# Two-block transformer kernel on one core: the second block's modulations made by TensorE in strips (layer 0) and by VectorE alone (last layer)

## The chip, the core and the metric

The kernel runs on one core of one Trainium2 chip. The core has a matrix engine (TensorE, PE in the profile, with its weight loads as PEld), a vector engine (VectorE, DVE), a scalar engine (ScalarE, ACT), GpSimd (POOL) and SyncE (SP), which issues most of the transfers. The metric is the device time of one execution in microseconds; lower is better.

## The reference, cut to what matters

A first block (three mixers, cross attention to `mem`, a convolutional feed-forward layer) is followed by a second block of two layers: attention and SwiGLU, then a recurrence (HGRN) and SwiGLU. Each layer of the second block is modulated: shifts, scales and gates for its 512 tokens come from the vector `c`, those for its 256 context tokens from `c_ctx`.

```python
for i in range(DEPTH_2):
    mod_l = (jax.nn.silu(c) @ ada_w[i] + ada_b[i])[:, None, :]           # 1024 -> 6 * 1024
    mod_c = (jax.nn.silu(c_ctx) @ ada_w[i] + ada_b[i])[None, None, :]
    sh1_l, sc1_l, gt1_l, sh2_l, sc2_l, gt2_l = jnp.split(mod_l, 6, axis=-1)
...
    hn_l = modulate(rms_norm_2(h, norm_mix_w[i]), sh1_l, sc1_l)           # h * (1 + sc) + sh
...
    h = h + gt1_l * y_l
    h = h + gt2_l * swiglu(modulate(rms_norm_2(h, norm_ffn_w[i]), sh2_l, sc2_l), ffn_w_in[i], ffn_w_out[i])
```

`ada_w` is 1024 x 6144 for each layer, 24 MiB in float32. Two vectors are multiplied with it, so a layer's modulations are two matrix-vector products.

## The kernel before

**Matrix products.** Activations lie with features on partitions. A product is made from two parts of each float32 operand, a high part of the reduced type `fp32r` and the rest: `Stream.weights` (L190) loads 128 columns of weights (512 KB) into one of three `raw` buffers, ScalarE rounds them to `wh` (L196), VectorE subtracts to give `wl` (L200), and `Stream.multiply` (L229) issues three `fp32r` products for each of the 8 tiles of the contraction (L236). `parts` has two buffers, so the weights of one tile are prepared while TensorE works on another. In a stage's last products (`closing`, L266) GpSimd makes half of each `wl`.

**Stages that the change touches.** The first block's feed-forward layer, `conv_ffn` (L1319), goes over 22 pairs of column tiles; each pair's two products pass ScalarE (L1331) and four VectorE steps (L1332, L1333), then the gate (L1349 to L1351) and the two parts (L335, L336); after 8, 8 and 6 pairs follow the products with `ffn_w_down`. The second block's layer 0 then has the projections, the attention `attend` (L1647), its output product, and `swiglu` (L1524), which is built as `conv_ffn` is, without the convolution and for 768 tokens. Layer 1's `swiglu`, the last stage, has the same for 512 tokens.

**The modulations.** `modulations(b, l, mod)` (L1458) is a generator; a step is one of 48 groups of 128 outputs, with the outputs on partitions and the 1024 inputs along the free dimension. It loads 512 KB of transposed weights `w` (L1477, two buffers) and makes a dot product with each of the two vectors, which are copied to all partitions. For layer 0 both go by GpSimd and ScalarE: GpSimd multiplies (L1484), ScalarE adds up (L1485). For layer 1 the first vector's product is one VectorE instruction with an accumulator (L1480); the second vector's, needed for the first 16 groups only, goes by GpSimd and ScalarE. Layer 0's run as `b.filler` beside `conv_ffn`, 2 or 3 steps for each pair of tiles (L1343), through `Context.steps` (L2022), which goes on to the context's first norm. Layer 1's run beside layer 0's `swiglu` (L1549). `Mod` (L1493) makes the norms' gains from the scales.

**Attention.** For each of 16 heads there are 7 steps: six with the 512 later tokens, one with the 256 context tokens. A step makes scores (L1719, L1720), the exponential (L1722), its two parts (L1728, L1729, on GpSimd, VectorE and ScalarE in turn) and, three steps later, the products with the values (L1741 to L1743). Beside them `ahead` (L1658) prepares the next two heads, with the queries' maxima sent by SP's queue (L1708, `q<-mr`), and `divide` (L1757) sends the sums by the same queue (L1760, `s<-sums`). Banks of PSUM for these side steps come from a pool `ps` of four. No weights are used between the projections and the output product.

**What sets the order.** A scheduler places the instructions when the program is built, by the order in which the generators are stepped, buffers and its own estimate of time. On each engine, and in SP's queue, they are then taken in that fixed order; one that waits holds back all behind it.

Of the kernel before, what the change touches and what calls it, by code (L numbers as in the profile page):

```python
# [26 lines left out]
# ---------------------------------------------------------------------------------------------  # L27
# Layout of the inputs, and constants of the shapes.


def _w(a):
    """[K, M] -> [M / 128, 128, K / 128, 128]: for each 128 columns, what each partition holds."""
    a = np.asarray(a)
    k, m = a.shape
    return np.ascontiguousarray(a.reshape(k // P, P, m // P, P).transpose(2, 1, 0, 3))


def _fm(a):
    """[tokens, features] -> [128, features / 128, tokens]."""
# [5 lines left out]
def _wt(a):  # L45
    """[K, M] -> [M / 256, K / 512, 128, 4, 256]."""
# [20 lines left out]
def _consts():  # L67
# [28 lines left out]
    out["half"] = np.full((P, 32), -0.5)  # L96
# [4 lines left out]
#: What all of the kernel needs, what the first block's mixers need, the second block's layers.  # L101
CGROUPS = {
    "all": ["ident", "half"],
# [6 lines left out]
def _layout(i):  # L110
# [26 lines left out]
    o["cc"] = np.ascontiguousarray(np.broadcast_to(np.stack([i["c_2"][0], i["c_ctx_2"]]), (P, 2, D)))  # L137
    o["ctx"] = _fm(i["ctx_2"][0])
    for l in range(2):
        o[f"ada{l}"] = np.ascontiguousarray(i["ada_w_2"][l].T.reshape(48, P, D))  # L140
        o[f"ffn_in{l}"] = _w(i["ffn_w_in_2"][l])
        o[f"ffn_out{l}"] = _w(i["ffn_w_out_2"][l])
# [26 lines left out]
# ---------------------------------------------------------------------------------------------  # L169


class Stream:
    """A stream of matrix products: its weights as loaded, their two parts, its accumulators."""
# [16 lines left out]
    def weights(self, src, ks, m=P, parts=None):  # L190
        """src [128, ks, m] in DRAM -> its high and low parts."""
# [11 lines left out]
    def accumulators(self, kinds):  # L203
        """For each (n, count): that many accumulators [128, n], of the same bank where they fit."""
# [12 lines left out]
    def products(self, W, ks, xs, n, ms, take, m=P, k0=0):  # L217
        """take(i, acc): acc [m, n] holds columns ms[i] of x W, features on partitions. A step for each i."""
# [6 lines left out]
    def product(self, src, ks, sets, m=P, k0=0):  # L225
        """For each (acc, xh, xl) of sets(k): acc += (rows k of the weights)^T x."""
# [1966 lines left out]
```

## Time and profile before

| what | value |
|---|---|
| three runs | 3298.18, 3301.41, 3302.06 us; median 3301.41 us |
| span of the profiled execution | 3296.8 us; what lies around it isn't in the profile, the median is 4.6 us above it |
| TensorE busy | 3096.2 us (94%) |
| VectorE, ScalarE, GpSimd busy | 1943.9, 1302.4, 1123.0 us |
| `conv_ffn`'s stretch read below | 953.6 to 1367.3 us |
| attention's stretch | 1540.2 to 1740 us |
| layer 0's `swiglu` beside the modulations | 1860 to 2050 us |
| layer 1's `swiglu`, same products as `conv_ffn` | 2906.2 to 3239.2 us |

The busy share of TensorE is an average over stages. A stretch is read by how much of it TensorE is not busy, by which engine ends those waits, and by the granted clock, of which the profile gives the share of full speed (2.4 GHz; the other level is 1.2 GHz).

### The profile page before, as it was taken

Reading aid. Unit: us, or ns where it says so; the run is one execution under the profiler, and the core shown is the slowest. Engines: PE = TensorE matmul, PEld = TensorE weight load, DVE = VectorE, ACT = ScalarE, POOL = GpSimd, SP = SyncE. Lnnn points to the kernel's source line nnn. Section 1 sums busy time; section 2 is a strip of 40 time slices with the busy share of each in tenths; the row PEclk is TensorE's granted clock in tenths of the full one; section 3 lists DMA queues with packets and bytes.
Section 4 is the critical chain, followed back from the end, with each engine's and each line's share of the span. In section 5 each row is a group of like instructions: output and inputs, shape, how many; then the busy total and the mean of one; then the engine's idle time right before and its main releaser. Section 6 shows DMA issues by size and latency. Waiting matters only on the chain.

```text
span 3296.8 us, 50925 instructions
## 1 busy us (share of the span) xinstructions
PE 3096.2 (94%) x20168; PEld 2640.3 (80%) x20168; DVE 1943.9 (59%) x3138; ACT 1302.4 (40%) x2333; POOL 1123.0 (34%) x942
## 2 busy tenths in 40 slices
PE   7999999989998889989999989999999999899998
PEld 6777777769796667888768968888889999788887
DVE  6454476456469695777975585333465555653334
ACT  4332234334345565544664331111344443332223
POOL 3222032230048988267975340000233232310003
PEclk9999999999999989999999999999999999989999
DMA  2111333234244444342003355221231111123333
GB/s 98 54 56 46 96 91 94 85 124 125 76 147 134 161 153 158 109 128 65 1 1 122 115 192 191 65 64 58 86 112 58 52 58 43 49 77 96 96 96 115
DMA packets 130911, 309.20 MB, mean 94 GB/s; under 512 B 33888, under 2 KB 55088, under 8 KB 130032
## 3 DMA queue, kind: packets, MB, share of 16 engines
q1 hardware_dynamic: 126032, 293.95, 28.6%
q10 hardware_dynamic: 4640, 12.00, 1.0%
q8 instruction: 158, 2.59, 0.3%
q14 instruction: 81, 0.66, 0.1%
HBM read 296.23 MB, written 8.39 MB: 92 GB/s over the span
## 4 chain that ended last, share of the span: by engine, by line
PE 68%; DVE 13%; POOL 6%; issue 5%; DMA 4%; ACT 3%; SPq 0%; POOLq 0%; DVEq 0%; ACTq 0%
PE acc L236 45%; DVE wl L200 4%; PE ps L520 3%; PE gate L1190 3%; POOL x L1484 2%; PE acc L258 2%; PE acc L259 2%; PE acc L260 2%; PE ps L1930 2%; DMA w<-in_ada_dram 2%; POOL pl L1729 1%; DVE t L1351 1%; DVE t L1350 1%; DVE junk L1480 1%; ACT wh L196 1%
## 5 line engine op out<-in xcount | busy, mean ns | idle before, releaser
L236 PE MATMUL acc<-hh,wl 128*128 128x512 f32 (+1 forms) x2296 | 772.5, 368 | 62.3 <-DVE wl L200 58.8
L236 PE MATMUL acc<-hh,wh 128*128 128x512 f32 (+1 forms) x2296 | 766.4, 365 | 0.0
L236 PE MATMUL acc<-hl,wh 128*128 128x512 f32 (+1 forms) x2296 | 764.2, 365 | 0.0
L200 DVE TENSOR_TENSOR wl<-raw,wh 128x1024 fp32r<-128x1024 f32 (+3 forms) x584 | 585.0, 1004 | 279.3 <-ACT wh L196 276.3
L196 ACT CAST wh<-raw 128x1024 fp32r<-128x1024 f32 (+4 forms) x584 | 479.9, 826 | 580.7 <-PE acc L236 356.4
L236 PEld LDWEIGHTS acc<-hh,wl 128*128 128x128 f32 x2296 | 408.3, 192 | 144.5 <-DVE wl L200 71.5
L200 POOL TENSOR_TENSOR wl<-raw,wh 128x512 fp32r<-128x512 f32 (+1 forms) x120 | 170.4, 1423 | 1014.5 <-ACT wh L196 579.9
L236 PEld LDWEIGHTS acc<-hh,wh 128*128 128x128 f32 x2296 | 407.1, 191 | 69.3 <-issue 1.1
L236 PEld LDWEIGHTS acc<-hl,wh 128*128 128x128 f32 x2296 | 407.5, 191 | 66.5 <-issue 0.8
L1484 POOL TENSOR_TENSOR x<-w,silu 128x1024 f32<-128x1024 f32 x112 | 323.7, 2918 | 46.1 <-ACT x L1485 23.0
L236 PE MATMUL acc<-mh,wl 128*128 128x512 f32 (+1 forms) x848 | 268.0, 341 | 26.7 <-DVE wl L200 26.4
L236 PE MATMUL acc<-mh,wh 128*128 128x512 f32 (+1 forms) x848 | 263.2, 336 | 0.0
L236 PE MATMUL acc<-ml,wh 128*128 128x512 f32 (+1 forms) x848 | 262.7, 335 | 0.4 <-DVE ml L336 0.4
L236 PEld LDWEIGHTS acc<-mh,wl 128*128 128x128 f32 x848 | 152.8, 191 | 51.0 <-DVE wl L200 33.6
L236 PEld LDWEIGHTS acc<-ml,wh 128*128 128x128 f32 x848 | 152.6, 190 | 19.1 <-DVE ml L336 1.7
L236 PEld LDWEIGHTS acc<-mh,wh 128*128 128x128 f32 x848 | 152.2, 190 | 17.1
L1509 DVE SCALAR_TENSOR_TENSOR X<-acc,mod,X 128x256 f32<-128x256 f32 (+1 forms) x112 | 65.6, 594 | 154.5 <-PE acc L236 154.5
L1557 ACT ACTIVATE t<-acc 128x512 f32<-128x512 f32 x66 | 34.5, 525 | 309.1 <-PE acc L236 307.8
L1485 ACT ACTIVATE x<-x 128x1024 f32<-128x1024 f32 x112 | 118.4, 1057 | 93.5 <-POOL x L1484 93.2
L1558 DVE SCALAR_TENSOR_TENSOR t<-t,acc 128x512 f32<-128x512 f32 x66 | 39.4, 596 | 169.2 <-ACT t L1557 169.1
L258 PE MATMUL acc<-wl,hh 128*128 128x256 f32 x448 | 126.8, 285 | 1.7 <-DVE wl L200 1.0
L259 PE MATMUL acc<-wh,hl 128*128 128x256 f32 x448 | 127.0, 284 | 0.0
(597 smaller groups left out, 6051.8 us busy)
## 6 DMA issues: line engine op xcount, KB each, us to landing
w<-in_ada_dram SPq DMA_DIRECT2D x96, 512.0 KB
raw<-in_ffn_in_dram SPq DMA_DIRECT2D x88, 512.0 KB
raw<-in_ffn_w_up_dram SPq DMA_DIRECT2D x44, 512.0 KB
raw<-in_ffn_out_dram SPq DMA_DIRECT2D x32, 512.0 KB
raw<-in_hg_w_dram SPq DMA_DIRECT2D x32, 512.0 KB
raw<-in_ffn_out_dram SPq DMA_DIRECT2D x40, 384.0 KB
raw<-in_w_qkv_dram SPq DMA_DIRECT2D x24, 512.0 KB
raw<-in_attn_wo_dram SPq DMA_DIRECT2D x24, 512.0 KB
```

Of the source, the lines that this page charges most:

```text
L196: nc.scalar.copy(h, raw)
L200: e.tensor_tensor(l[:, s], raw[:, s], h[:, s].bitcast(F32), op=ALU.subtract)
L236: nc.tensor.matmul(z[0], w[:, k], z[x], start=k == 0 and n == 0, stop=k == ks - 1 and n == 2)
L258: nc.tensor.matmul(acc, xh, wl, start=k == 0, stop=False)
L259: nc.tensor.matmul(acc, xl, wh, start=False, stop=False)
L260: nc.tensor.matmul(acc, xh, wh, start=False, stop=k == ks - 1)
L520: nc.tensor.matmul(out(r, ci), lhsT(r, ci), rhs(r, ci), start=start, stop=stop)
L1190: nc.tensor.matmul(acc, w[:, 0], x, start=k + i == 0, stop=k == 7 and i == 2)
L1484: nc.gpsimd.tensor_tensor(x, w, c[:, n], op=ALU.mult)
L1485: nc.scalar.activation(x, x, AF.Identity, accum_out=sums[:, g, n : n + 1])
L1509: return lambda i, acc: b.nc.vector.scalar_tensor_tensor(X[:, i], acc, gate[:, i : i + 1], X[:, i], op0=ALU.mult, op1=ALU.add)
L1930: nc.tensor.matmul(p[:, c], kc[:, c * P : (c + 1) * P], qc[:, c * P : (c + 1) * P], start=True, stop=True)
```

## The change

Layer 0's modulations are now matrix products. `silu` of the two vectors is put on partitions as a [128, 8, 32] tile, of which two columns are used and 30 are zero. A group is 512 outputs, 12 groups in all: 8 float32 products with a 128 x 32 stationary tile (`silu`) and 512 moving columns of weights, one for each tile of the contraction, into four strips of 32 PSUM partitions by `tile_position`. The weights come in four transfers of 512 KB for a group. ScalarE copies the bank, and four small products with `sel` add the strips and turn the outputs to partitions; VectorE adds the bias. Four groups (parts 0 and 1 of the modulations) run beside `conv_ffn`, one step for every second pair; eight run inside `attend`, a step for every seventh of its steps, and take their weights through the stream's three `raw` buffers and their bank from the pool of four. The last layer's modulations take VectorE for both vectors, with three buffers for `w`. The gain of the second norm is made later, by `second()`.

```diff
-    out["half"] = np.full((P, 32), -0.5)
+    out["half"] = np.full((P, 8), -0.5)
+    out["sel"] = p[:, None] % 32 == np.arange(2)[None]
...
-        o[f"ada{l}"] = np.ascontiguousarray(i["ada_w_2"][l].T.reshape(48, P, D))
+        ada = i["ada_w_2"][l]
+        o[f"ada{l}"] = np.ascontiguousarray(ada.T.reshape(48, P, D) if l else
+                                            ada.reshape(4, 2, P, 12, 512).transpose(3, 0, 2, 1, 4))
...
-                b.fill(2 + m % 2)
+                b.fill(m % 2)
...
+class Products:
+    def __init__(self, b, mod, pool, small):
+        self.b, self.mod = b, mod
+        nc = b.nc
+        self.silu = pool.tile([P, 8, 32], F32, name="silu")
+        c, t = (small.tile([P, 8, 2], F32, name=n) for n in ("cin", "cth"))
+        nc.scalar.dma_start(c, b.a["ck"])
+        nc.gpsimd.memset(self.silu, 0.0)
+        nc.scalar.activation(t, c, AF.Tanh, scale=0.5)
+        nc.vector.tensor_scalar(t, t, 0.5, 0.5, op0=ALU.mult, op1=ALU.add)
+        nc.vector.tensor_tensor(self.silu[:, :, :2], c, t, op=ALU.mult)
+    def steps(self, groups, bank, pool):
+        b, nc = self.b, self.b.nc
+        bias = b.v["ada_b_2"]
+        for g in groups:
+            acc = bank()
+            for k in range(8):
+                if k % 2 == 0:
+                    w = pool.tile([P, 2, 512], F32, tag="raw", name="ada")
+                    nc.sync.dma_start(w, b.a["ada0"][g, k // 2])
+                c = 32 * (k % 4)
+                nc.tensor.matmul(acc[c : c + 32], self.silu[:, k], w[:, k % 2], start=k < 4, stop=k >= 4,
+                                 tile_position=(0, c))
+            yield
+            sb = pool.tile([P, 512], F32, tag="raw", name="mods")
+            nc.scalar.copy(sb, acc)
+            for j in range(4):
+                nc.tensor.matmul(acc[:, 2 * j : 2 * j + 2], sb[:, j * P : (j + 1) * P], b.c["sel"], start=j == 0,
+                                 stop=j == 3)
+            s = slice(4 * g, 4 * g + 4)
+            nc.vector.tensor_tensor(self.mod[:, s], acc[:, :8].rearrange("p (j n) -> p j n", n=2),
+                                    bias[:, s].unsqueeze(2).to_broadcast([P, 4, 2]), op=ALU.add)
+            yield
...
-        p2 = b.pool("ad2", 2, ctx=ctx, side="right")
+        p2 = b.pool("ad2", 3, ctx=ctx, side="right")
...
-        nc.gpsimd.tensor_scalar(t, t, 0.5, 0.5, op0=ALU.mult, op1=ALU.add)
-        nc.gpsimd.tensor_tensor(c, c, t, op=ALU.mult)
+        nc.vector.tensor_scalar(t, t, 0.5, 0.5, op0=ALU.mult, op1=ALU.add)
+        nc.vector.tensor_tensor(c, c, t, op=ALU.mult)
...
-            for n in range(2 if l == 0 or g < 16 else 1):
-                if n == 0 and l:
-                    nc.vector.scalar_tensor_tensor(t[:, 0], w, 1.0, c[:, n], op0=ALU.mult, op1=ALU.mult,
-                                                   accum_out=sums[:, g, n : n + 1])
-                    continue
-                x = p2.tile([P, D], F32, tag="x", name="x")
-                nc.gpsimd.tensor_tensor(x, w, c[:, n], op=ALU.mult)
-                nc.scalar.activation(x, x, AF.Identity, accum_out=sums[:, g, n : n + 1])
+            for n in range(2 if g < 16 else 1):
+                nc.vector.scalar_tensor_tensor(t[:, 0], w, 1.0, c[:, n], op0=ALU.mult, op1=ALU.mult,
+                                               accum_out=sums[:, g, n : n + 1])
...
+        if i % 7 == 3:
+            next(more, None)
...
-        yield from modulations(b, 0, self.mod[0])
+        with ExitStack() as c:
+            self.products = Products(b, self.mod[0], cx, b.pool("cin", 1, ctx=c, side="right"))
+            ps, ada = b.pool("psad", 1, PSUM, ctx=c), b.pool("ada", 4, ctx=c, side="right")
+            yield from self.products.steps(range(4), lambda: ps.tile([P, 512], F32, tag="ps", name="mods"), ada)
...
+                more = old_.products.steps(range(4, 12), lambda: ps.tile([P, 512], F32, tag="ps", name="mods"), st.raw)
+                att = attend(b, Q, K2, V, o, high, low, at2, ps, c, more)
```

How the instructions stand is shown at three places. In the changed file the same code has other line numbers: L204 for L200, L240 for L236, L382 for L378, L351 for L347, L1754 for L1708, L1806 for L1760, L1765 and L1766 for L1719 and L1720, L1787 to L1789 for L1741 to L1743.

GpSimd in the stretch of `conv_ffn`, before: `x<-w,silu` is layer 0's product with a vector, on both sides of it stand its help with the weights' parts and the norms' sums.

```order
L200 TENSOR_TENSOR wl<-raw,wh 128x512 x5
L347 TENSOR_TENSOR rs<-rs,ct_all 128x2
L1470 TENSOR_SCALAR junk<-junk 128x2048
L1471 TENSOR_TENSOR silu<-silu,junk 128x2048
L1484 TENSOR_TENSOR x<-w,silu 128x1024 x96
L378 TENSOR_TENSOR sum<-sum,sq 128x256 x2
L347 TENSOR_TENSOR rs<-rs,ct_all 128x2
```

The same place after:

```order
L204 TENSOR_TENSOR wl<-raw,wh 128x512 x5
L351 TENSOR_TENSOR rs<-rs,ct_all 128x2
L1473 MEMSET silu 128x256
L382 TENSOR_TENSOR sum<-sum,sq 128x256 x2
L351 TENSOR_TENSOR rs<-rs,ct_all 128x2
```

The 96 products and the two steps for `silu` are gone from GpSimd; one memset stands in their place, and the engine has nothing else in this stretch.

TensorE in `attend`, before: `st` are scores, `acc` the products with the values, `sc` those for the maxima of the next heads.

```order
L1698 MATMUL sc<-K_13074,q_15043 128x384 x2
L1719 MATMUL st<-q_14780,K_14166 128x512
L1720 MATMUL st<-q_14778,K_13074 128x512
L1698 MATMUL sc<-K_13074,q_15043 128x384
L1719 MATMUL st<-q_14780,K_14166 128x512
L1720 MATMUL st<-q_14778,K_13074 128x512
```

The same place after, for the second of the eight groups: `mods<-ada,silu` are the products in strips.

```order
L1744 MATMUL sc<-K_12780,q_14773 128x384 x2
L1489 MATMUL mods<-ada,silu 32x512 x6
L1744 MATMUL sc<-K_12780,q_14773 128x384
L1765 MATMUL st<-q_14486,K_13872 128x512
L1766 MATMUL st<-q_14484,K_12780 128x512
...
L1744 MATMUL sc<-K_12780,q_14773 128x384
L1489 MATMUL mods<-ada,silu 32x512 x2
L1765 MATMUL st<-q_14486,K_13872 128x512
L1766 MATMUL st<-q_14484,K_12780 128x512
...
L1789 MATMUL acc<-ph,Vh 65x512
L1495 MATMUL mods<-ct_all,mods 128x2 x4
L1744 MATMUL sc<-K_12780,q_14774 128x384 x2
```

Six strips stand together, the last two 13 rows behind them, the four small products 15 rows further on; all are in TensorE's fixed order among the scores.

SP's queue in `attend`, before, with what each transfer waits for:

```order
L187 DMA raw<-in_attn_wo_dram 128x1024 [waits DMAHW4_49,DVE_49,Pool_49]
L1708 DMA q_14780<-mr 1x6x128 [waits Activation_49]
L1708 DMA q_14781<-mr 1x6x128
L1760 DMA s<-sums 6x1x128 [waits DVE_49,Activation_49,Pool_49]
L1760 DMA s<-sums 6x1x128 [waits DMAHW5_49,Activation_49]
L1760 DMA s<-sums 6x1x128 [waits DMAHW6_49,Activation_49]
```

After:

```order
L1487 DMA ada<-in_ada_dram 128x1024 [waits DMAHW3_49,PE_49]
L1487 DMA ada<-in_ada_dram 128x1024 [waits DMAHW5_49,PE_49]
L1487 DMA ada<-in_ada_dram 128x1024 [waits DMAHW0_49,PE_49]
L1487 DMA ada<-in_ada_dram 128x1024 [waits DMAHW4_49,PE_49,Activation_49]
L1806 DMA s<-sums 6x1x128 [waits DVE_49,Activation_49,Pool_49]
L1754 DMA q_14486<-mr 1x6x128 [waits Activation_49]
L1754 DMA q_14487<-mr 1x6x128 [waits DMAHW6_49]
L1806 DMA s<-sums 6x1x128 [waits DMAHW7_49,Activation_49]
L1487 DMA ada<-in_ada_dram 128x1024 [waits DMAHW1_49,PE_49]
```

The last transfer of a group and the first three of the next one now stand between the small transfers of the attention, and wait for TensorE (the strips that free a buffer) and once for ScalarE.

## Rows read from the trace of the kernel before

**Rows 1.** The page, part 1: engines, busy us and share of the span.

```profile
PE 3096.2 (94%) x20168; PEld 2640.3 (80%) x20168; DVE 1943.9 (59%) x3138; ACT 1302.4 (40%) x2333; POOL 1123.0 (34%) x942
```

**Rows 2.** Busy time by stretch: length, engines, granted clock, DMA share, GB/s.

```profile
953.60:1367.30 413.70, 363.88 (x1618) 293.54 (x1617) 314.95 (x280) 232.57 (x368) 294.58 (x109) 0.95 0.45 145
2906.20:3239.20 333.00, 331.32 (x1547) 278.89 (x1548) 137.66 (x173) 90.45 (x123) 2.97 (x4) 0.98 0.29 89
1540.20:1740.00 199.80, 188.58 (x907) 135.44 (x907) 155.95 (x263) 126.82 (x250) 176.35 (x178) 0.95 0.01 4
1860.00:2050.00 190.00, 170.54 (x936) 147.18 (x935) 133.97 (x176) 50.38 (x78) 57.18 (x18) 0.96 0.57 188
```

**Rows 3.** Groups by line, 965 to 1310 us: busy, mean ns, idle before.

```profile
L1484 POOL TENSOR_TENSOR x<-w,silu 128x1024 f32<-128x1024 f32 x96 | 273.9, 2883 | 30.8 <-ACT x L1485 21.7 <-DMA w<-in_ada_dram 8.9
...
L200 DVE TENSOR_TENSOR wl<-raw,wh 128x1024 fp32r<-128x1024 f32 x47 | 85.1, 1814 | 24.5 <-ACT wh L196 24.5
...
L1351 DVE TENSOR_TENSOR t<-t,u 128x512 f32<-128x512 f32 x16 | 41.7, 2603 | 0.0
```

**Rows 4.** The same view, 2880 to 3297 us, layer 1's `swiglu`.

```profile
L200 DVE TENSOR_TENSOR wl<-raw,wh 128x1024 fp32r<-128x1024 f32 (+2 forms) x79 | 84.9, 1075 | 21.2 <-ACT wh L196 21.0
...
L1559 DVE TENSOR_TENSOR t<-t,acc 128x512 f32<-128x512 f32 x22 | 15.1, 688 | 55.7 <-PE acc L236 55.7
```

**Rows 5.** Waits of TensorE, 953 to 1368 us: us, times, longest.

```profile
PE acc L236 <- DVE wl L200: 49.6, 28, 5.7
```

**Rows 6.** The chain of waits in order of time: start, us, what.

```profile
968.08 26.52 PE acc L236 x180
...
1329.17 38.13 PE acc L236 x168
...
1375.18 4.45 DMA raw<-in_ffn_w_down_dram
```

**Rows 7.** TensorE in order of time, first block's recurrence: start, us, instruction.

```profile
238.13 0.80 PE L520 MATMUL pp<-bt,AR 64*64 64x64 f32 x21
238.86 1.12 PE L555 MATMUL pp<-twd,up 64*128 64x512 f32 x2
239.91 0.50 PE L1190 MATMUL gate<-hh,wl 128*128 128x512 f32 x1
240.25 0.39 PE L1190 MATMUL gate<-hl,wh 128*128 128x512 f32 x1
240.47 0.40 PE L1190 MATMUL gate<-hh,wh 128*128 128x512 f32 x1
240.80 0.33 PE L520 MATMUL ps<-S,GT 64*64 64x64 f32 x4
```

**Rows 8.** Line 555, 100 to 250 us: ns min/median/max of one.

```profile
L555 PE MATMUL pp<-twd,up x4: 589/641/693, 151.1 to 239.4; 64*128 64x512 f32 x4
```

**Rows 9.** TensorE in order of time: small products, 2 moving columns.

```profile
1424.64 0.95 PE L342 MATMUL ss<-ones,sum 128*128 128x2 f32 x8
1425.45 1.03 PE L342 MATMUL ss<-ones,sq 128*128 128x2 f32 x8
```

**Rows 10.** Waits of TensorE in attention, 1540 to 1741 us.

```profile
PE acc L1741 <- POOL pl L1729: 3.9, 10, 0.7
...
PE st L1719 <- DMA q<-mr: 2.1, 1, 2.1
```

**Rows 11.** Waits, 1860 to 2050 us, layer 0's `swiglu`.

```profile
DVE junk L1480 <- DMA w<-in_ada_dram: 32.5, 24, 3.3
...
PE acc L236 <- DVE wl L200: 19.3, 6, 7.0
```

**Rows 12.** Line 1480, the last layer's products on VectorE.

```profile
L1480 DVE SCALAR_TENSOR_TENSOR junk<-w,silu x48: 1210/1225/3426, 1879.2 to 2035.6; 128x1024 f32<-128x1024 f32 x48
```

**Rows 13.** Busy time by stretch, as rows 2, in layer 0's `swiglu`.

```profile
1900.00:1950.00 50.00, 39.43 (x203) 33.74 (x204) 46.40 (x45) 21.02 (x37) 32.53 (x11) 0.90 0.53 181
1950.00:2000.00 50.00, 47.54 (x260) 40.72 (x259) 33.74 (x59) 9.92 (x15) 0.00 (x0) 0.97 0.72 240
```

More of the change, by code (lines that the diff above doesn't have):

```diff
@@ L102 @@
 CGROUPS = {
-    "all": ["ident", "half"],
+    "all": ["ident", "half", "sel"],
     "mix": ["hsel", "bones", "cmat", "id64", "mnr", "ma", "up0", "lo0", "up", "causal", "run"],
@@ L1452, in block1, with modulations @@
     return X, h, late
-def modulations(b, l, mod):
+class Products:
[31 more added lines that the diff above has]
+            yield
+def modulations(b, mod):
     nc = b.nc
@@ L1476, in modulations @@
             w = p2.tile([P, D], F32, tag="w", name="w")
[L1477 to L1485 removed]
+            nc.sync.dma_start(w, b.a["ada1"][g])
+            for n in range(2 if g < 16 else 1):
+                nc.vector.scalar_tensor_tensor(t[:, 0], w, 1.0, c[:, n], op0=ALU.mult, op1=ALU.mult,
+                                               accum_out=sums[:, g, n : n + 1])
             if g % 8 == 7:
[L1487 removed]
+                s = slice(g - 7, g + 1), slice(0, 2 if g < 16 else 1)
                 nc.vector.tensor_tensor(mod[:, *s], mod[:, *s], sums[:, *s], op=ALU.add)
@@ L1496, in __init__, with gain, second @@
     def __init__(self, b, mod, l, kind):
-        nc = b.nc
-        part = lambda n: mod[l][:, 8 * n : 8 * n + 8, kind]
-        gains = []
-        for n, sc, w in ((1, 1, "norm_mix_w_2"), (2, 4, "norm_ffn_w_2"))[: 1 if l and kind else 2]:
-            g = b.cp.tile([P, 8], F32, name=f"g{n}_{l}{kind}")
-            nc.vector.scalar_tensor_tensor(g, part(sc), 1.0, b.v[w][:, 8 * l : 8 * l + 8], op0=ALU.add, op1=ALU.mult)
-            gains.append(g)
-        self.sh1, self.g1, self.gt1 = part(0), gains[0], part(2)
-        self.sh2, self.g2, self.gt2 = part(3), gains[-1], part(5)
+        self.b, self.l, self.kind = b, l, kind
+        part = self.part = lambda n: mod[l][:, 8 * n : 8 * n + 8, kind]
+        self.g1 = self.gain(1, 1, "norm_mix_w_2")
+        self.sh1, self.gt1 = part(0), part(2)
+        self.sh2, self.gt2 = part(3), part(5)
+    def gain(self, n, sc, w):
+        g = self.b.cp.tile([P, 8], F32, name=f"g{n}_{self.l}{self.kind}")
+        self.b.nc.vector.scalar_tensor_tensor(g, self.part(sc), 1.0, self.b.v[w][:, 8 * self.l : 8 * self.l + 8],
+                                              op0=ALU.add, op1=ALU.mult)
+        return g
+    def second(self):
+        self.g2 = self.gain(2, 4, "norm_ffn_w_2")
+        return self
 def add_gated(b, X, gate):
@@ L1644, in keys, with attend @@
                 nc.vector.tensor_tensor(l, r, h.bitcast(F32), op=ALU.subtract)
-def attend(b, Q, K2, V, out, high, low, p2, psc, ctx):
+def attend(b, Q, K2, V, out, high, low, p2, psc, ctx, more):
     nc = b.nc
@@ L1801, in attend @@
                 next(parts.pop())
+    run(more)
 def lower_bounds(b, pool):
@@ L2023, in steps @@
         b = self.b
-        yield from modulations(b, 0, self.mod[0])
+        cx = b.pool("cx", 1, ctx=self.c, side="right")
+        with ExitStack() as c:
+            self.products = Products(b, self.mod[0], cx, b.pool("cin", 1, ctx=c, side="right"))
+            ps, ada = b.pool("psad", 1, PSUM, ctx=c), b.pool("ada", 4, ctx=c, side="right")
+            yield from self.products.steps(range(4), lambda: ps.tile([P, 512], F32, tag="ps", name="mods"), ada)
         self.mods = [Mod(b, self.mod, 0, k) for k in range(2)]
-        self.X = b.pool("cx", 1, ctx=self.c, side="right").tile([P, 8, n], F32, name="Xc")
+        self.X = cx.tile([P, 8, n], F32, name="Xc")
         b.nc.scalar.dma_start(self.X, b.a["ctx"])
@@ L2084, in block2 @@
             c.close()
+            for m in mods:
+                m.second()
             hp = b.pool("hn2", 1, ctx=ctx)
@@ L2099, in block2 @@
     with ExitStack() as c:
-        b.filler = modulations(b, 1, old_.mod[1])
+        b.filler = modulations(b, old_.mod[1])
         def then():
@@ L2110, in block2 @@
     cw.close()
-    m = parts[0].mod
+    m = parts[0].mod.second()
     def wo(o, k0, k1, p):
```

6 lines of the change are left out of this document (2 added, 4 removed).

## The prediction

> **What bounds the kernel now.** I read the page's engine line first: TensorE is busy for 94% of the span [rows 1], so what can be won is what it isn't busy for, and what makes it slower while it is. The busy times by stretch show where [rows 2]. `conv_ffn` takes 413.7 us; layer 1's `swiglu`, which has the same products, takes 333.0. In `conv_ffn` GpSimd is busy for 294.6 us, in the other for 3.0. The groups by line say what GpSimd does there, the 96 products `x<-w,silu` of 2883 ns, and what VectorE's steps cost beside them: `wl` 1814 ns, the gate's last step 2603 [rows 3]; without GpSimd's work like steps take 1075 and 688 [rows 4]. (The latter sum holds some smaller forms, so the ratio is a little less than it looks.) The waits give the consequence: TensorE stands 49.6 us for `wl` from VectorE [rows 5]. And the chain of waits shows the same loop without the disturbance: 26.5 us at its start and 38.1 at its end of products without a gap, while GpSimd has nothing to multiply [rows 6]. So `conv_ffn` is bound by VectorE, slowed by GpSimd, and by TensorE at the rest. In attention, TensorE is busy for 188.6 of 199.8 us, so 11.2 us are free there, and the transfers stand idle, 1% [rows 2].
>
> **The change: `conv_ffn` freed of GpSimd.** The most to be had is 413.7 − 333.0 = 80.7 us. `conv_ffn` has 1618 matmuls against 1547; 71 more at about 0.11 us (the 26.5 us of rows 6 over 180 products come to 0.15 for each; many of the 71 are shorter) are 8 us that stay. I take **−73**; the ends are −49.8 (only the gaps, 413.7 − 363.9) and −80.7. TensorE's busy time is above the other stretch's too, since a matmul that is issued late, behind a wait, is shown longer; that is why I don't take the lower end. ScalarE's additions (L1485) and 32 of 48 transfers leave as well; neither is what TensorE waits for.
>
> **The price of a group of strips.** A group is 8 float32 products of 512 columns and 4 small ones. No row of before has a 128 x 32 stationary tile. The nearest by columns is line 555: a product is two instructions, which begin 1.05 us before the next instruction (238.86 to 239.91 [rows 7]); one takes 0.59 to 0.69 from start to end [rows 8], so they overlap by a little, and half a product is 0.42 to 0.52. I take 0.44. Do strips run beside each other? The only products at different places of the array are line 520's, 64 x 64, on other rows and other columns: 21 take 0.80 us from the first's start to the last's end [rows 7], 38 ns for each at most, where half a float32 product of 64 columns, one after the other, would take 64/512 of 0.42 to 0.52, 53 to 66 ns. So two places do run side by side there. In TensorE's fixed order the two halves of a strip go to the same place and must follow each other; the second half can only run beside the first half of the next strip. So 6 strips take 7 steps and the last 2 take 3: 10 x 0.44 = 4.4 us. Four small products: eight of the like take 0.81 [rows 9], so 0.4, and with the wait for ScalarE's copy hidden behind other rows 0.81 for all. Changes between strips and full products: the gate's product before line 520 begins 0.33 before it, 0.11 more than the step before [rows 7]; four of these are 0.4. **A group is 5.6 us**; one after the other it would be 8 x 1.05 + 1.2 = 9.6; four at a time (16 halves in 4 to 6 steps) 3.8.
>
> The Trainium skill, "TensorE: Matmul & The Clock Gate", Part 3, states that a weight load overlaps products in flight only where the row group differs; all strips here use all rows, which would make the group 9.6. The same section reports 2.38 times the speed for three strips of 32 columns, which would make it nearer 4. Rows 7 can't tell, since line 520 changes both rows and columns.
>
> **Put into `conv_ffn`:** 4 groups, 22 us, and 2 us for waits on their bank and copies; the stage is then bound by TensorE, so all of it counts. Net −73 + 22 + 2 = **−49** (one after the other −33, four at a time −56).
>
> **Put into attention:** 8 groups, 45 us. Of a group's four transfers the last one waits until a `raw` buffer is free, that is until the first strips have run, and lands 4.45 us after it is issued (the like transfer of rows 6). The last two strips stand 13 rows behind the six, some 3 us; half a microsecond to one and a half of wait for each group, with what else fills it 4 us in all. What TensorE waits for now are small things, GpSimd's and VectorE's `pl` and one transfer `q<-mr` [rows 10], and the 11.2 us that it isn't busy are cover: while it does strips, those engines get ahead. 45 + 4 − 11 = **+38**. Ends: +19 (four at a time, no wait, all cover) and +89 (one after the other, no cover, one wait each). 32 transfers of 512 KB in 200 us are 84 GB/s, and the kernel moves 240 elsewhere [rows 13], so the bandwidth isn't short. The small `q<-mr` and `s<-sums` stand behind these transfers in SP's queue; I give them nothing of their own, since `ahead` works two heads ahead, and price the opposite below. The output product's weights are loaded later, but the last group is 14 steps, 25 us, ahead of them.
>
> **Layer 0's `swiglu`:** its 190 us have 19.5 without TensorE, 19.3 of it for `wl` [rows 2, 11]. The last layer's 16 second products move from GpSimd to VectorE, 16 x 1.225 us = 20 us [rows 12], on an engine that is busy for 134 of 190. VectorE's own waits are for transfers (32.5 us, rows 11), a third buffer helps there. Where GpSimd has work, 1900 to 1950, TensorE is busy for 39.4 of 50 us; where it has none, 47.5 [rows 13]. I take **−12**, between 0 (VectorE's extra time eats it) and −19.5. The rest costs nothing: the 32 columns of `silu` and the memset lie on idle engines, `second()` is a few columns moved to a place behind attention.
>
> **Sum:** −49 + 38 − 12 = −23. The span of 3296.8 becomes 3274, and with the 4.6 us by which the median is above it **3278 us**. It hangs on the size of a group: with a group of g, the sum is −90 + 12 g, and at g = 7.5 us nothing is left.
>
> **The rivals.**
> *One strip after another* (slower side). If TensorE can't load a strip's weights while another strip in the same rows runs, a group is 9.6 us: −33 + 70 − 12 = +25, **3327 us**. For it: line 555's halves, on one set of rows, overlap little [rows 7, 8]; it decides from 7.5 us for a group. Against it: line 520.
> *Four at a time.* If the two halves of a strip are not held to their order or halves are short, 3.8 us: −56 + 23 − 12 = −45, **3256 us**.
> *Attention waits for its transfers.* SP's queue is in fixed order; a `q<-mr` behind a transfer that waits for TensorE comes late, or the last two strips wait the whole landing: 4.45 us for each of 8 groups, of which 0.5 are counted, +32 more: +9, **3310 us**. For it: one `q<-mr` already makes TensorE wait 2.1 us [rows 10], and the strips hold one of the pool's four banks for 28 rows. Against: TensorE's waits on transfers there are few.
> *`conv_ffn` isn't freed.* If VectorE is slow for reasons of its own, the −73 are missing: +24 + 38 − 12 = +50, **3351 us**. Against: rows 6.
>
> **How the numbers follow.** Pairs 0.45, one after the other 0.25, four at a time 0.17, waits in attention 0.10, not freed 0.03. A measurement of this kernel can tell some 0.2%, 6.6 us, from no change. Pairs is faster with 0.87 of its chance (its terms are unsure by some 15 us), the same with 0.10; four at a time is faster; one after the other is slower but for 0.01; waits are split 0.2, 0.35, 0.45. Faster 0.39 + 0.17 + 0.02, some 0.59; same 0.045 + 0.01 + 0.035, 0.09; slower the other 0.32. The range goes from 3250, where four at a time has its lower part left out (0.05), to 3332, above one after the other by 5 us (0.1 and the not freed 0.03 left out). The cases of faster alone reach from 3250 to 3295.
>
> **What the changed profile would show.** The stretch of `conv_ffn` at 365 us, `wl` near 1.1 us, TensorE's wait for `wl` under 10 us: the first term. The starts of the `mods<-ada,silu` instructions: 0.44 us for each strip's step says pairs, 1.05 for a strip one after another, 0.25 four at a time. Attention at 238 us, with TensorE's waits on `ada` transfers and `q<-mr` together under 6 us; above 30 the third rival. Layer 0's `swiglu` with waits for `wl` under 10 us. The prediction is wrong if the groups by line show `wl` as slow as before, or a group above 7.5 us.

## The result, and the profile after

Four runs of the changed kernel took 3249.3 to 3259.6 us, median **3253.6 us**; before it was 3301.7 us in runs beside them. The ratio is 0.9861, with a 95% interval from 0.9847 to 0.9875: 48 us, 1.4% faster. The forecast was 3278 us, its range 3250 to 3332. The profiled execution has a span of 3247.5 us, 49.3 less than before.

The page's engine line, part 1, as [rows 1]: TensorE is busy for 96%, GpSimd and ScalarE have lost 345 and 112 us of work.

```profile
PE 3114.1 (96%) x20456; PEld 2645.7 (81%) x20456; DVE 1827.2 (56%) x3179; ACT 1190.2 (37%) x2121; POOL 778.1 (24%) x827
```

Busy time by stretch of the changed kernel, columns as in [rows 2]: `conv_ffn` to its last `u`, attention from the first scores to the last products with the values, and 190 us of layer 0's `swiglu` beside the modulations.

```profile
962.70:1323.60 360.90, 357.05 (x1706) 289.20 (x1705) 201.92 (x277) 130.76 (x178) 12.97 (x12) 1.00 0.37 116
...
1496.10:1713.10 217.00, 210.04 (x1098) 143.00 (x1099) 159.66 (x275) 133.38 (x259) 171.11 (x178) 0.98 0.26 84
1834.00:2024.00 190.00, 187.75 (x1069) 162.96 (x1068) 133.20 (x217) 35.61 (x49) 0.00 (x0) 1.00 0.60 197
```

`conv_ffn` went from 413.7 to 360.9 us and is now nearly all TensorE. Attention went from 199.3 (with the same ends) to 217.0. In the third row TensorE has 1069 products in 190 us where it had 936.

Groups by line and TensorE's waits in `conv_ffn`, the answers to [rows 3] and [rows 5]:

```profile
L204 DVE TENSOR_TENSOR wl<-raw,wh 128x1024 fp32r<-128x1024 f32 (+1 forms) x59 | 70.7, 1202 | 9.6 <-ACT wh L200 9.5
L1355 DVE TENSOR_TENSOR t<-t,u 128x512 f32<-128x512 f32 x20 | 13.7, 685 | 0.0
```

```profile
PE acc L240 <- DVE wl L204: 6.8, 8, 2.3
```

`wl` fell from 1814 to 1202 ns, the gate's last step from 2603 to 685, and the wait for `wl` from 49.6 to 6.8 us.

TensorE in order of time (start, us, instruction), the first whole group of strips in `conv_ffn` and what follows:

```profile
1003.48 1.91 PE L1489 MATMUL mods<-ada,silu 128*32 128x512 f32 x12
1005.32 0.50 PE L240 MATMUL acc<-hh,wl 128*128 128x512 f32 x1
...
1007.62 1.05 PE L1489 MATMUL mods<-ada,silu 128*32 128x512 f32 x4
1008.60 0.50 PE L240 MATMUL acc<-hh,wl 128*128 128x512 f32 x1
```

Six strips (12 instructions, two halves each) take 1005.32 − 1003.48 = 1.84 us, two strips 0.98: together 2.82 us, against 4.4 in the forecast's pairs and 2.6 in its rival of four at a time. With the small products, 0.79 in the chain of waits, a group is 3.6 us.

From the first starts of lines in both traces, the stages differ by:

| stage (from, to) | before | after | difference |
|---|---|---|---|
| start to `conv_ffn`'s first `g` | 978.5 | 987.5 | +9.0 |
| to the first product of the second block's projections | 439.0 | 386.0 | −53.0 |
| to the first scores | 122.7 | 122.6 | −0.1 |
| attention | 199.3 | 217.0 | +17.7 |
| to layer 0's first gate | 103.6 | 104.4 | +0.8 |
| layer 0's `swiglu`, to the recurrence | 629.4 | 604.0 | −25.4 |
| the rest | 824.3 | 826.0 | +1.7 |

### The profile page after: what moved, and what is told of

The parts are those of the page before. It is cut to its first block, busy times and chain, and to the rows that moved or that the text cites. A ratio compares the mean times of both kernels' runs of the same rounds, so it can differ in the third digit from the quotient of the medians.

```text
span 3247.5 us, 51132 instructions
## 1 busy us (share of the span) xinstructions
PE 3114.1 (96%) x20456; PEld 2645.7 (81%) x20456; DVE 1827.2 (56%) x3179; ACT 1190.2 (37%) x2121; POOL 778.1 (24%) x827
## 4 chain that ended last, share of the span: by engine, by line
PE 83%; DVE 8%; issue 2%; DMA 2%; ACT 2%; POOL 2%; SPq 0%; DVEq 0%; POOLq 0%; ACTq 0%
PE acc L240 57%; DVE wl L204 3%; PE ps L524 3%; PE gate L1194 3%; PE acc L262 2%; PE acc L263 2%; PE acc L264 2%; PE ps L1979 2%; PE mods L1489 1%; PE ss L346 1%; ACT wh L200 1%; PE sc L1744 1%; PE st L1765 1%; DMA w<-in_ada_dram 1%; PE st L1766 1%
## 5 line engine op out<-in xcount | busy, mean ns | idle before, releaser
L240 PE MATMUL acc<-hh,wl 128*128 128x512 f32 (+1 forms) x2296 | 761.7, 364 | 7.8 <-DVE wl L204 5.6
L240 PE MATMUL acc<-hh,wh 128*128 128x512 f32 (+1 forms) x2296 | 757.9, 361 | 0.0
L240 PE MATMUL acc<-hl,wh 128*128 128x512 f32 (+1 forms) x2296 | 757.2, 361 | 0.0
L200 ACT CAST wh<-raw 128x1024 fp32r<-128x1024 f32 (+4 forms) x584 | 480.4, 826 | 650.4 <-PE acc L240 412.4
L204 DVE TENSOR_TENSOR wl<-raw,wh 128x1024 fp32r<-128x1024 f32 (+3 forms) x584 | 555.6, 954 | 254.5 <-ACT wh L200 248.0
L204 POOL TENSOR_TENSOR wl<-raw,wh 128x512 fp32r<-128x512 f32 (+1 forms) x120 | 169.9, 1419 | 1295.6 <-ACT wh L200 583.3
L240 PEld LDWEIGHTS acc<-hh,wl 128*128 128x128 f32 x2296 | 402.5, 189 | 85.5 <-DVE wl L204 9.4
L240 PEld LDWEIGHTS acc<-hh,wh 128*128 128x128 f32 x2296 | 402.4, 189 | 68.3 <-issue 0.9
L240 PEld LDWEIGHTS acc<-hl,wh 128*128 128x128 f32 x2296 | 402.1, 189 | 65.5 <-issue 0.8
L240 PE MATMUL acc<-mh,wl 128*128 128x512 f32 (+1 forms) x848 | 265.9, 339 | 15.4 <-DVE wl L204 14.9
L240 PE MATMUL acc<-mh,wh 128*128 128x512 f32 (+1 forms) x848 | 260.6, 332 | 0.0
L240 PE MATMUL acc<-ml,wh 128*128 128x512 f32 (+1 forms) x848 | 260.2, 332 | 0.2 <-DVE ml L340 0.2
L240 PEld LDWEIGHTS acc<-mh,wl 128*128 128x128 f32 x848 | 150.9, 188 | 37.8 <-DVE wl L204 19.9
L240 PEld LDWEIGHTS acc<-ml,wh 128*128 128x128 f32 x848 | 151.4, 189 | 17.6 <-DVE ml L340 0.4
L240 PEld LDWEIGHTS acc<-mh,wh 128*128 128x128 f32 x848 | 150.9, 188 | 17.4
L264 PE MATMUL acc<-wh,hh 128*128 128x256 f32 x448 | 126.7, 285 | 0.0
L1605 DVE TENSOR_TENSOR t<-t,acc 128x512 f32<-128x512 f32 x66 | 39.4, 598 | 137.4 <-PE acc L240 136.9
```

The source lines that it names most:

```text
L200: nc.scalar.copy(h, raw)
L204: e.tensor_tensor(l[:, s], raw[:, s], h[:, s].bitcast(F32), op=ALU.subtract)
L240: nc.tensor.matmul(z[0], w[:, k], z[x], start=k == 0 and n == 0, stop=k == ks - 1 and n == 2)
L264: nc.tensor.matmul(acc, xh, wh, start=False, stop=k == ks - 1)
L1605: nc.vector.tensor_tensor(t, t, u, op=ALU.mult)
```

## The experiments

All times are medians, each beside runs of the kernel before on the same chip; the ratio is to those. The kernel before had medians of 3300.0 to 3303.9 us in the four sets, so between rows the ratios are the safer comparison: GpSimd's products, for one, cost 12 us by the medians and 7 by the ratios.

| run | us | ratio, 95% interval | `conv_ffn` | attention |
|---|---|---|---|---|
| changed kernel | 3253.6 | 0.9861, 0.9847 to 0.9875 | 386.0 | 217.0 |
| one strip | 3306.9 | 1.0005, 0.9992 to 1.0017 | 405.0 | 255.1 |
| two by two | 3263.9 | 0.9873, 0.9848 to 0.9897 | 389.1 | 226.6 |
| no groups in attention | 3231.4 | 0.9784, 0.9756 to 0.9812 | 384.5 | 199.7 |
| GpSimd's products back | 3265.8 | 0.9883, 0.9861 to 0.9906 | 399.3 | 218.6 |
| ScalarE's sums back | 3254.8 | 0.9868, 0.9849 to 0.9886 | 388.6 | 218.3 |
| last layer undone | 3278.1 | 0.9944, 0.9924 to 0.9964 | 386.8 | 217.1 |
| two buffers | 3260.5 | 0.9889, 0.9870 to 0.9908 | 385.3 | 217.1 |
| even strips | 3247.2 | 0.9848, 0.9830 to 0.9866 | 383.4 | 220.3 |
| products and sums, chained | 3273.1 | 0.9913, 0.9895 to 0.9931 | 406.6 | 218.4 |
| products and sums, apart | 3269.3 | 0.9904, 0.9883 to 0.9925 | 409.2 | 218.3 |
| first block's order as before | 3241.8 | 0.9822, 0.9805 to 0.9839 | 386.1 | 218.7 |
| even strips and that order | 3237.1 | 0.9803, 0.9785 to 0.9821 | 384.3 | 217.6 |

The last two columns are us of the one profiled execution, by the ends of the table above. The run without groups in attention leaves out results that are needed; it is there for its time alone.

### One strip after another

```diff
-                c = 32 * (k % 4)
-                nc.tensor.matmul(acc[c : c + 32], self.silu[:, k], w[:, k % 2], start=k < 4, stop=k >= 4,
-                                 tile_position=(0, c))
+                nc.tensor.matmul(acc[:32], self.silu[:, k], w[:, k % 2], start=k == 0, stop=k == 7,
+                                 tile_position=(0, 0))
...
-            nc.scalar.copy(sb, acc)
+            nc.scalar.copy(sb[:32], acc[:32])
...
```

> All eight products of a group go to one strip of 32 partitions, one after the other; the copy and the four small products take that strip alone. If the strips of the changed kernel run beside each other (16 halves in 6 steps, 1.84 + 0.98 us), the same 16 halves now take 16 steps of 0.43 us, 6.9 us: +4.1 us for each group, +16 in conv_ffn, +33 in attention, about 3302 us. If a product is short only because its stationary tile is narrow, and places don't matter: within 5 us of 3254.

It took 3306.9 us: the whole gain is gone. TensorE in order of time, the same place:

```profile
1003.39 5.34 PE L1488 MATMUL mods<-ada,silu 128*32 128x512 f32 x12
1008.66 0.50 PE L240 MATMUL acc<-hh,wl 128*128 128x512 f32 x1
...
1010.03 1.90 PE L1488 MATMUL mods<-ada,silu 128*32 128x512 f32 x4
1011.87 0.50 PE L240 MATMUL acc<-hh,wh 128*128 128x512 f32 x1
```

Twelve halves now take 5.27 us, 0.44 each, in place of 1.84; four take 1.84 in place of 0.98. So half a product is 0.44 us, as the prediction took it, and the strips at different places do run beside each other, though all of them use all rows. Over 12 groups (5.27 + 1.84 − 2.82) x 12 is 51 us, the measured loss 53 (48 by the ratios).

### Two by two

```diff
-                c = 32 * (k % 4)
+                c = 32 * (k // 2)
-                nc.tensor.matmul(acc[c : c + 32], self.silu[:, k], w[:, k % 2], start=k < 4, stop=k >= 4,
+                nc.tensor.matmul(acc[c : c + 32], self.silu[:, k], w[:, k % 2], start=k % 2 == 0, stop=k % 2 == 1,
```

> The eight products go to the strips in the order 0, 0, 1, 1, 2, 2, 3, 3 instead of 0, 1, 2, 3, 0, 1, 2, 3. If TensorE begins a product only after all ahead of it in its queue have begun, three pairs take 10 steps of 0.43 us and the last pair 4, some 6.1 us for a group instead of 2.8: +3.3 each, +13 in conv_ffn and +26 in attention, about 3293 us. If it reaches past products that wait for their place, the six take 4 steps still and the last two 4: +0.8 each, about 3263 us.

3263.9 us, the second case. The six strips (0, 0, 1, 1, 2, 2) and then the two (3, 3):

```profile
1004.75 1.98 PE L1489 MATMUL mods<-ada,silu 128*32 128x512 f32 x12
1006.65 0.50 PE L240 MATMUL acc<-hh,wl 128*128 128x512 f32 x1
...
1008.94 1.90 PE L1489 MATMUL mods<-ada,silu 128*32 128x512 f32 x4
1010.77 0.50 PE L240 MATMUL acc<-hh,wl 128*128 128x512 f32 x1
```

Twelve halves at three places take 1006.65 − 1004.75 = 1.90 us, four steps, though neighbours in the program's order have the same place. If a half that waits for its place kept all behind it from starting, these would have been ten steps, 4.4 us. So halves further back start before it. That is the step of the prediction that failed, and an exception to what is said ahead of it, that one instruction that waits holds back all behind it.

### No groups in attention

```diff
-                more = old_.products.steps(range(4, 12), lambda: ps.tile([P, 512], F32, tag="ps", name="mods"), st.raw)
+                more = iter(())
```

> The eight groups in attention are left out with their 32 transfers; the modulations of parts 2 to 5 are the bias alone. If their price is TensorE's time less the waits that they fill, attention becomes as long as in the kernel before, some 200 us from the first scores to the output product's first weights, and the kernel some 18 us shorter, about 3236 us. If the transfers in SP's queue or the bank also cost, the gain is 29 us (the groups' whole time) or more: 3225 or less.

3231.4 us, 22 less. Attention's stretch, to compare with the second row of the changed kernel:

```profile
1496.40:1696.10 199.70, 188.12 (x906) 135.59 (x907) 156.37 (x263) 126.24 (x249) 175.77 (x178) 0.95 0.01 4
```

Without groups attention has its length of before, 199.7 us, with 11.6 us in which TensorE isn't busy. Eight groups of 3.6 us are 28.9; they made it 17.3 longer. That the difference is 11.6, just what stood idle, is chance: with the groups TensorE is still not busy for 7.0 us (217.0 − 210.0 in the changed kernel's second row), so only 4.6 of the idle time were filled. The other 7.0 are in TensorE's busy time, which grew by 21.9 us (188.1 to 210.0) and not by 28.9: attention's own 906 products took less time, at a granted clock of 0.98 instead of 0.95. Waits for the transfers add next to nothing: in the changed kernel TensorE waited once for `q<-mr`, 1.7 us, and its weight loads once for `ada`, 0.4.

### What slowed `conv_ffn`: GpSimd's products, ScalarE's sums

In two runs 32 transfers of 512 KB were put back beside `conv_ffn`, with 96 instructions on them, by GpSimd in the first and by ScalarE in the second; nothing uses their results. They are spread over 18 pairs, and the strips' steps stay at every second pair.

```diff
+            for m in range(18):
+                for j in range(2 if m % 9 < 7 else 1):
+                    x = ew.tile([P, 2, 512], F32, tag="extw", name="extw")
+                    b.nc.sync.dma_start(x, b.a["ada0"][m % 12, j])
+                    for _ in range(3):
+                        b.nc.gpsimd.tensor_tensor(x, x, x, op=ALU.mult)
...
+                        b.nc.scalar.activation(x, x, AF.Identity, accum_out=es)
```

> The changed kernel, and beside conv_ffn 32 more transfers of 512 KB with three GpSimd products of 128 x 1024 on each, 96 in all, whose results nothing uses; ScalarE adds up nothing. If GpSimd's work by itself slows VectorE, wl goes back to 1.6 to 1.8 us, the gate's last step to 2.6 or more, and conv_ffn grows by 45 to 75 us: 3300 to 3330 us. If ScalarE's additions were the cause: under +10, and wl near 1.1 us.

> As the run with GpSimd's products, with the same 32 more transfers, but ScalarE makes 96 sums of 128 x 1024 on them (about 0.9 us each) and GpSimd nothing. If GpSimd alone slowed VectorE, wl stays near 1.1 us and the kernel within 10 us of 3254 us. If ScalarE's additions or the transfers did it, conv_ffn grows by 40 us or more, 3294 us or more.

ScalarE's sums (1.06 us each) and the transfers cost nothing that can be told (3254.8). GpSimd's products cost 12 us, 13 in `conv_ffn`'s column, far under the 45 to 75 of the expectation, though they slow VectorE nearly as expected. Durations by line (ns minimum, median, maximum), 1010 to 1250 us, first of the kernel before, then of this run:

```profile
L1350 DVE SCALAR_TENSOR_TENSOR t<-t,g x13: 2858/2884/2896, 1010.5 to 1244.8; 128x512 f32<-128x512 f32 x13
L1332 DVE SCALAR_TENSOR_TENSOR u<-acc,vt,u x13: 735/736/740, 1013.3 to 1247.6; 128x511 f32<-128x511 f32 x13
L336 DVE SCALAR_TENSOR_TENSOR ml<-t,mh x12: 692/2112/2126, 1019.4 to 1240.3; 128x512 fp32r<-128x512 f32 x12
```

```profile
L2085 POOL TENSOR_TENSOR extw<-extw x91: 1887/2336/2887, 1009.7 to 1248.6; 128x1024 f32<-128x1024 f32 x91
L1354 DVE SCALAR_TENSOR_TENSOR t<-t,g x13: 680/2377/2381, 1019.7 to 1223.7; 128x512 f32<-128x512 f32 x13
L340 DVE SCALAR_TENSOR_TENSOR ml<-t,mh x14: 1599/1601/2123, 1013.8 to 1229.9; 128x512 fp32r<-128x512 f32 x14
```

The mean `wl` of this run is 1524 ns in the groups by line, the median 1470, and TensorE's waits for it in 962 to 1380 us are 15.5. For one pair of tiles VectorE needs two steps `t`, four with `acc`, one `ml` and two `wl`. By medians that is before 2 x 2.88 + 4 x 0.74 + 2.11 + 2 x 1.95 = 14.7 us, here 2 x 2.38 + 4 x 0.74 + 1.60 + 2 x 1.47 = 12.3, in the changed kernel 7.5. TensorE's 48 products of a pair take 10.9 (0.228 us each). Only what goes beyond that can show, 3.8 us a pair before and 1.4 here. So two thirds of the slowdown should have brought back over a third of the cost; they brought back a fifth, 13 of 67 us. The sum explains why the cost is not in proportion, not its size.

The kernel before had one thing more: ScalarE's sums waited for GpSimd's products, with `wh` behind them. Two runs put products and sums back together, once so that each sum takes a product's result, once so that it takes a tile of its own (in both, `silu` lies in 48 columns to make room):

```diff
+                        b.nc.gpsimd.tensor_tensor(x, w, w, op=ALU.mult)
+                        b.nc.scalar.activation(x, x, AF.Identity, accum_out=es)
...
+                        b.nc.scalar.activation(ea, ea, AF.Identity, accum_out=es)
```

> The changed kernel with 32 more transfers beside conv_ffn, 96 GpSimd products (128 x 1024, into two buffers of their own) and, as in the kernel before, ScalarE's sum of each product: 96 of about 1.24 us that wait for GpSimd in ScalarE's queue. The products alone made conv_ffn 13 us longer, the sums alone 3. If conv_ffn suffers because ScalarE waits for GpSimd with the wh casts queued behind it, this brings back most of the rest: conv_ffn 45 to 65 us longer, about 3305 us. If the two loads only add up: 16 us, about 3270.

> The same transfers and products, and the same 96 sums on ScalarE, at like places of its queue, of a tile that GpSimd doesn't write, so that no sum waits for a product. If the wait in ScalarE's queue is the cause: conv_ffn 15 to 25 us longer than in the changed kernel, 3270 to 3280 us, well under the chained run. If the loads of the two engines together are the cause: as the chained run.

They took 3273.1 and 3269.3 us, with intervals that overlap: the wait in ScalarE's queue wasn't the cause here. But the chained run didn't rebuild that wait. ScalarE's waits from 985 to 1310 us, before and in the chained run:

```profile
ACT x L1485 <- POOL x L1484: 64.9, 51, 7.5
```

```profile
ACT extx L2089 <- POOL extx L2088: 11.9, 14, 1.6
```

Of the 67 us by which `conv_ffn` was longer before (53.0, and 14.4 for the four groups that it now has), the runs brought back 13 by products alone and 21 to 23 with sums. The remaining 45 **stay open**, for the kernel before differed in at least three things that no run rebuilt. A product read two different tiles (`w` and `silu`) and took 2852 ns in the median, and the last began at 1301 us; in these runs it read one tile twice, took 2222 to 2338, and the last began at 1246 to 1258. The wait in ScalarE's queue was as long as the rows above say. And VectorE's steps for the modulations (`mod`, L1488) used the results, in the same fixed order as `wl`. In the chain of waits of before, 1180 to 1240 us, where pairs of tiles are worked on, over 80% is VectorE, and a pair takes some 15 us as in the sum. Over 985 to 1310 us a quarter of the chain goes along GpSimd's products themselves, mostly at the products with `ffn_w_down`; in the chains of the runs above they have no such part. The two chains, first of 1180 to 1240 us, then of 985 to 1310:

```profile
by line: DVE wl L200 27.6%; DVE t L1351 18.8%; DVE t L1350 18.6%; DVE ml L336 10.6%; issue 8.6%; DVE g L1332 4.6%; DVE u L1332 4.5%; ACT mh L335 4.2%; ACT x L1485 1.7%; ACT g L1331 1.1%; DVE g L1333 0.4%; DVE u L1333 0.4%
```

```profile
by line: POOL x L1484 24.1%; issue 17.4%; DVE wl L200 15.4%; DVE t L1351 10.4%; DVE t L1350 9.5%; DVE ml L336 4.8%; PE acc L236 3.0%; DVE u L1332 2.5%; DVE g L1332 2.4%; ACT mh L335 2.4%; ACT x L1485 1.9%; DMA w<-in_ada_dram 1.4%; DMA Xc<-i
```

### The last layer's modulations

The second vector back on GpSimd and ScalarE, with two buffers; and VectorE for both with two buffers:

```diff
+                if n == 0:
+                    nc.vector.scalar_tensor_tensor(t[:, 0], w, 1.0, c[:, n], op0=ALU.mult, op1=ALU.mult,
+                                                   accum_out=sums[:, g, n : n + 1])
+                    continue
+                x = p2.tile([P, D], F32, tag="x", name="x")
+                nc.gpsimd.tensor_tensor(x, w, c[:, n], op=ALU.mult)
+                nc.scalar.activation(x, x, AF.Identity, accum_out=sums[:, g, n : n + 1])
```

```diff
-        p2 = b.pool("ad2", 3, ctx=ctx, side="right")
+        p2 = b.pool("ad2", 2, ctx=ctx, side="right")
```

> The changed kernel with the last layer's modulations as before: the second vector's products by GpSimd and ScalarE for 16 groups, two buffers. If the 24.6 us that layer 0's swiglu is shorter by come from there, they come back: about 3278 us. If they come from attention's end or from the clock after it: within 10 us of 3254.

> The changed kernel with two buffers for the last layer's weights in place of three; both vectors by VectorE. If the third buffer is what ends VectorE's waits for transfers, half or more of the 24.6 us come back, 3266 us or more. If the gain is GpSimd's and ScalarE's work that is gone: within 4 us of 3254.

3278.1 and 3260.5 us: all of the 25 us come from this part. Some 7 of them come from the third buffer by the medians, between the two cases of its expectation; the interval overlaps that of the changed kernel, but the profile shows a loss too. In the 190 us from 1834 us on TensorE has 1069 products in the changed kernel, 917 with the part undone and 1025 with two buffers:

```profile
1834.00:2024.00 190.00, 170.27 (x917) 146.09 (x916) 134.62 (x177) 50.88 (x79) 56.49 (x18) 0.95 0.58 186
```

```profile
1834.00:2024.00 190.00, 181.29 (x1025) 157.10 (x1025) 133.50 (x220) 35.36 (x50) 0.00 (x0) 0.98 0.60 192
```

The waits there: the changed kernel, then the part undone, then two buffers (to 2030):

```profile
DVE junk L1523 <- DMA w<-in_ada_dram: 12.6, 10, 2.7
```

```profile
DVE junk L1524 <- DMA w<-in_ada_dram: 35.5, 24, 3.3
...
PEld acc L240 <- DVE wl L204: 22.6, 9, 7.0
```

```profile
DVE junk L1523 <- DMA w<-in_ada_dram: 36.7, 29, 2.9
...
PEld acc L240 <- DVE wl L204: 10.1, 5, 3.5
```

With two buffers VectorE waits for transfers as long as before, 36.7 us, but TensorE's weight loads wait for `wl` only 10.1 instead of 22.6. The mean `wl` is 1608 ns with the part undone and 1220 with two buffers: an engine that is at 70% has room for its own waits once nobody slows its steps. Whether GpSimd's products alone do that here, or ScalarE's sums too, was not tried apart.

### The first block's order

> The changed kernel with a tile of constants that is as wide as before (the vectors' silu laid out in 48 columns instead of 256 makes room), so that TensorE has the first block's products in the order of the kernel before. If the 8 us that the first block is longer by in all runs of the changed kernel come from that order: 3246 us, the first block back at 907 us. If they are chance or come from elsewhere: 3254.

```diff
-    out["half"] = np.full((P, 8), -0.5)
+    out["half"] = np.full((P, 30), -0.5)
...
-        self.silu = pool.tile([P, 8, 32], F32, name="silu")
+        self.silu = pool.tile([P, 48], F32, name="silu")
...
-                nc.tensor.matmul(acc[c : c + 32], self.silu[:, k], w[:, k % 2], start=k < 4, stop=k >= 4,
+                nc.tensor.matmul(acc[c : c + 32], self.silu[:, 2 * k : 2 * k + 32], w[:, k % 2], start=k < 4, stop=k >= 4,
```

(A strip's other 30 rows then hold sums that `sel` leaves out.) 3241.8 us, 12 less than the changed kernel, clear of noise, and `conv_ffn`'s first `g` at 979.3 us, against 986.2 to 992.6 in all eleven profiles with the narrower constants (the last run of the study, with the same width, has it at 983.4). Besides that width only the layout of `silu` differs, and the two runs with that layout and the narrower constants, products with sums, have 986.2 and 990.0. In the traces the sequence of TensorE's products in the first block is that of the kernel before, but for a few, in this run, and another in the changed kernel. That the width does this through the scheduler's estimate for the load of the constants is argued, not shown. Where the order costs, 700 to 760 us of the changed kernel, of this run and of the kernel before:

```profile
700.00:760.00 60.00, 50.47 (x191) 38.47 (x191) 31.64 (x35) 18.61 (x31) 17.58 (x13) 0.83 0.36 119
```

```profile
700.00:760.00 60.00, 52.13 (x222) 40.73 (x223) 38.08 (x49) 22.47 (x40) 18.14 (x13) 0.97 0.43 136
```

```profile
700.00:760.00 60.00, 52.45 (x224) 41.08 (x225) 38.65 (x50) 22.85 (x40) 17.70 (x12) 0.97 0.42 136
```

191 products at a granted clock of 0.83 against 222 and 224 at 0.97: with the new order TensorE spends more of this stretch at the lower of its two levels, 1.2 GHz.

### Even portions of strips

```diff
+            for k in (0, 1, 2, 3, 4, 5, 6, 7) if g < 4 else (0, 1, 2, 3, 6, 7, 4, 5):
...
+                if k == 3 and g < 4:
+                    yield
...
-                b.fill(m % 2)
+                b.fill(1)
```

> The same products, in other portions: in attention four strips and four instead of six and two, in conv_ffn eight together for three of the four groups. By steps of 0.43 us a group goes from 6 steps to 4 (0.98 + 0.98 us, or 1.84, in place of 2.82): -0.9 us each, -3 in conv_ffn and -7 in attention, about 3244 us. If attention is bound by what feeds the scores, only conv_ffn's part is left, about 3250 us.

> Both together: strips in even portions and the first block in the order of the kernel before. 3247 less 8, about 3239 us; if the first block's order costs nothing, 3247.

Eight strips together take four steps, 1.85 us, as six did with 1.84:

```profile
1026.38 1.92 PE L1491 MATMUL mods<-ada,silu 128*32 128x512 f32 x16
1028.23 0.50 PE L240 MATMUL acc<-hh,wl 128*128 128x512 f32 x1
```

3247.2 us alone and 3237.1 with the first block's order, 6 and 5 less than without; the intervals overlap with those of the kernels without it, so this gain isn't shown, and the profile of the first has attention 3 us longer, not shorter. Both parts together make the fastest kernel of the study that computes everything, 0.9803 (0.9785 to 0.9821) of before, clear of the changed kernel's 0.9847.

## Why the prediction was right, and where it wasn't

The direction and the range held; the size was short by 25 us, and the time fell near the rival of four at a time (3256), not on pairs. That it came so near, and that the range held, is in part luck: layer 0's `swiglu` gave 13 us more than was taken, and the first block, which was put at nothing, cost 9. With the first block's order as before the time is 3241.8, outside the range. By its steps:

- **`conv_ffn` freed, −73:** −67 (−53.0, and 14.4 for its groups), between its ends. That VectorE was the bound, and GpSimd what slowed it, holds for the pairs of tiles; but only 13 us were brought back by products and 21 to 23 with sums. The prediction read the chain of waits at its two ends [rows 6]; between them a quarter of it goes along GpSimd's own products, which the prediction doesn't speak of.
- **A group, 5.6 us:** measured 3.6. The half of 0.44 us was right. The step that failed is that the two halves of a strip, in their order, hold up what stands behind them, ten steps for a group; the runs show six, since halves further back start first and four places work at a time. The Trainium skill's sentence that a weight load overlaps products in flight only where the row group differs ("TensorE: Matmul & The Clock Gate", Part 3), which the prediction weighed for one strip after another, isn't borne out: six strips on the same rows take 1.84 us at four places and 5.27 at one, and in the trace weight loads for them begin while the first strips' products run.
- **Groups in `conv_ffn`, +24:** 14.4 by the rows, four groups of 3.6. Net −53 against −49.
- **Attention, +38:** +17.7. The group's size took 16 off, and the 4 us of waits didn't come. The cover of 11 us came out at 11.6 by luck: the strips filled 4.6 us of idle time, and 7.0 came from attention's own products, which took less time. The transfers between `q<-mr` and `s<-sums` in SP's queue did no harm: TensorE waited 1.7 us for `q<-mr`, 2.1 in [rows 10].
- **Layer 0's `swiglu`, −12, at most −19.5:** −25.4, beyond the end. The end counted only the time that TensorE isn't busy [rows 11]; but TensorE's busy time for a product fell too, from 0.182 to 0.176 us, and the granted clock rose from 0.96 to 1.00. That is the very point for which the prediction didn't take `conv_ffn`'s lower end.
- **"The rest costs nothing":** the first block cost 9.0 us in the profile of the changed kernel. The narrower constants stand in the diff, and the prediction didn't ask what they do to the order of work that the change doesn't touch.

## What to carry to other kernels

Give column strips of a float32 product different places in turn, in portions of four or eight: each portion of four takes two steps of half a product (by the rows; a gain in time from even portions isn't shown here). Where a stage is bound by an engine that another one slows, sum that engine's steps for one turn of the loop and compare with the bound's: only the excess shows; here two thirds of the slowdown cost a fifth of the time. Then follow the chain of waits through the whole stage, for the disturbing engine can be a bound of its own. And in a program whose order is made by a scheduler, compare the order of the stages that a change doesn't touch; a tile of constants that was 22 columns narrower cost 12 us here, 8 of them in the first block.

## What the runs showed of the hardware

A VectorE step that reads two tiles of SBUF gets longer beside GpSimd's products. By medians `t<-t,g` takes 2884 ns beside products of 2852, 2377 beside products of 2336, and 684 without them; `ml<-t,mh` 2112, 1601 and 693; `wl<-raw,wh` 1946, 1470 and 1217. Only the first lasts as long as the product beside it. A step of nearly the same size that reads PSUM and one tile of SBUF (`u<-acc,vt,u`) stays at 736 to 750. The Trainium skill, "SBUF — State Buffer", section "Who interferes with whom", says that a VectorE instruction with two SBUF inputs contends with a GpSimd instruction that reads SBUF, and calls the port pair that they share an exclusive lock; these rows agree with the first, and don't show by themselves which of the two waits. Strips of 32 columns that share all 128 rows run four at a time: six take 1.84 us at four places and 5.27 at one. Halves at a busy place are passed by (1.90 us where ten steps would be 4.4), and eight strips (1.85 us) cost what six do.
